# Reordering the first loads of an eight-core decoder trunk: modulation tiles in 1 MB transfers, half of x first, weight slabs gated, write-backs late

## The chip, the cores and the metric

The kernel runs on the 8 cores of one Trainium2 chip, one batch element on each core. Nothing passes between cores. The time is that of the slowest core, in microseconds (us); each quoted time of a run adds about 2 us to the span of its slowest core. Cores 0 to 3 are one die, cores 4 to 7 the other. The kernel issues its transfers from two queues, that of the SP engine and that of the POOL engine, and both use the core's 16 DMA engines (on the page of the kernel before, SP's queue takes 30.9% of their time and POOL's 20.2%).

Every execution lists the span and the mean granted TensorE clock of each core. In some executions one die, or both, are granted a lower clock and the run takes some per cent longer: the state *slow*. One run of the control took 6626 us, with cores 4 to 7 at 0.809 to 0.811; its cores 0 to 3 had 0.973 to 0.974. Fast runs are compared with fast runs. There is a second way to compare: a core shares no data with the others, so the cores of a die that was not slowed can be read even when the other die was (cores 0 to 3 of that run took 5689.7 to 5703.8 us, those of the control's two fast runs 5679.0 to 5704.1).

## The reference

Four layers, each a token mixer and a SwiGLU feed-forward, each with a modulated RMSNorm in front. What matters here is that nothing can start before the modulation of layer 0 is known, and that the modulation is a product of a vector with a 1024 x 6144 matrix.

```python
c_act = jax.nn.silu(c)                                   # (B, D)
for i in range(DEPTH):
    mod = jnp.einsum("bd,de->be", c_act, ada_w[i]) + ada_b[i]   # (B, 6D)
    sh1, sc1, g1, sh2, sc2, g2 = [m[:, None, :] for m in jnp.split(mod, 6, axis=-1)]
    h = rmsnorm(x, norm_mix_g[i]) * (1.0 + sc1) + sh1
    ...                                                  # layer 0: short gated convolution
    x = x + g1 * y
    h = rmsnorm(x, norm_ffn_g[i]) * (1.0 + sc2) + sh2
    x = x + g2 * swiglu(h, ffn_w_in[i], ffn_w_out[i])
```

## The kernel before

x is handled in four *passes* of 1024 positions, each in two halves of 512 (`nt` 0 and 1). Layer 0's mixer is ten weight slabs ("units") long; each slab serves both halves. In pass 0 a slab comes from HBM as f32, is cast to bf16 by the transfer on the POOL queue, and is written back to HBM as bf16 by the SP queue for the later passes:

```python
def load_slab(g):
    ...
    if s == 0 and (i, p) == (0, "M"):
        P.op("pool", lambda e: e.dma_start(out=wring[:, k, 0:L], in_=wsrc(i, p, q)), writes=[wb[k]], ...)
        P.op("sp", lambda e: e.dma_start(out=wdst(i, p, q), in_=wring[:, k, 0:L]), reads=[wb[k]], ...)
```

There are four slots in the ring. The modulation weights come as tiles of 128 x 512 f32 (256 KB); VectorE multiplies each with the activation and sums it (`ada_mul`). Layer 0's first two sections, 32 tiles, must be done before the first norm; the other 64 tiles of layer 0 are spread over the passes (16 in pass 0, 48 in passes 1 and 2) through a ring of three buffers. The conversions of layer 0's feed-forward weights to bf16 (`conv_tasks`, HBM to HBM, 19 slabs) are spread over the passes too. The start:

```python
issue_loads()                      # slabs 0 to 3 on POOL's queue, their write-backs on SP's
pre0[0]()                          # x, first half
for t in range(22):                # 22 modulation tiles, 256 KB each, on SP's queue
    ada_dma(0, t, hid2[...], ..., q="sp")
pre0[1]()                          # x, second half
for fn in pre0[2:12]: fn()         # squares and rstd of both halves
for t in range(22): ada_mul(0, t, ...)
for fn in ada_tasks(0, range(22, 32)): fn()    # 10 more tiles through the ring of three
...
for fn in pre0[12:]: fn()          # 16 norms
```

Of the kernel before, what the change touches and what calls it, by code (L numbers as in the profile page):

```python
# [7 lines left out]
F32 = mybir.dt.float32  # L8
# [13 lines left out]
LAG = 1  # L22
# [46 lines left out]
def _slab_table():  # L69
    tab = {}  # L70
    src = 0
    dst = 0
    for i in range(4):
        for part in (("B1", "B2", "B3", "F") if i % 3 == 1 else ("M", "F")):
            rows = []
            for name, L in _sub_slabs(i, part):
                if name == "bconv":
                    rows.append((name, L, None, dst))
                else:
                    rows.append((name, L, src, dst))  # L80
                    src += L * 128
                dst += L * 128
            tab[(i, part)] = rows
    return tab, src, dst

SLABS, TOTW, TOTB = _slab_table()
# [171 lines left out]
SECTIONS = (1, 0, 2, 4, 3, 5)  # L258
NCV = 10

def build():
# [4 lines left out]
    adaw = nc.dram_tensor("adaw", [4, NEH, 128, 512], F32, kind="ExternalInput").ap()  # L266
# [7 lines left out]
    P = Prog()  # L274
    es = contextlib.ExitStack()
    with es:
# [3 lines left out]
        xres = sb("xres", [128, 2, 8, NT], F32)  # L280
        hbuf = sb("hbuf", [128, 2, 8, NT], BF16)
        hid2 = sb("hid", [128, FC * NT], BF16)
        wring = sb("wring", [128, NRING, SLOT], BF16)
# [39 lines left out]
        xb = [[[Buf(f"x{b}_{c}_{t}") for t in range(2)] for c in range(8)] for b in range(2)]  # L323
        hb = [[[Buf(f"h{b}_{c}_{t}") for t in range(2)] for c in range(8)] for b in range(2)]
        hidb = [[Buf(f"hid{c}_{t}") for t in range(2)] for c in range(FC)]
        scrb = [Buf(f"scr{k}") for k in range(5)]
        wb = [Buf(f"w{k}") for k in range(NRING)]
        wdb = {(i, p, q): Buf(f"wd{i}{p}{q}") for (i, p), rows in SLABS.items() for q in range(len(rows))}
# [36 lines left out]
        def vcol(name, c=0, w=1):  # L365
            o = VOFF[name] + c
            return vecs[:, o:o + w]
# [35 lines left out]
        def wsrc(i, part, q):  # L403
            name, L, src, dst = SLABS[(i, part)][q]
            return wpack[src:src + 128 * L].rearrange("(p l) -> p l", p=128)

        def wdst(i, part, q):
            name, L, src, dst = SLABS[(i, part)][q]
            return wbf[dst:dst + 128 * L].rearrange("(p l) -> p l", p=128)
# [14 lines left out]
            cvstate["hist"].append(b)  # L424

        seq = []
        wstate = dict(loaded=0, used=0, done=0)

        def load_slab(g):
            i, p, s, q = seq[g]  # L430
            name, L, src, dst = SLABS[(i, p)][q]
            k = g % NRING
            if s == 0 and (i, p) == (0, "M"):
                P.op("pool", lambda e: e.dma_start(out=wring[:, k, 0:L], in_=wsrc(i, p, q)), writes=[wb[k]], sem=f"wc{k}", inc=16)
                P.op("sp", lambda e: e.dma_start(out=wdst(i, p, q), in_=wring[:, k, 0:L]), reads=[wb[k]],
                     writes=[wdb[(i, p, q)]], sem=f"wr{k}", inc=16)
            elif s == 0 and name == "bconv":
                def mkconv(e):
                    for gg in range(2):
                        ins = e.tensor_tensor(  # L440
                            wring[:, k, gg * CW:(gg + 1) * CW].rearrange("p (d c q) -> p d c q", c=32, q=4),
                            cmask[:, :].unsqueeze(1).unsqueeze(3).broadcast_to([128, NSH, 32, 4]),
                            wtab[:, 2 * q + gg, :, :].unsqueeze(2).broadcast_to([128, NSH, 32, 4]), ALU.mult)
                    return ins

                P.op("dve", mkconv, reads=[wtabb, convcb], writes=[wb[k]])
                P.op("sp", lambda e: e.dma_start(out=wdst(i, p, q), in_=wring[:, k, 0:L]), reads=[wb[k]],
                     writes=[wdb[(i, p, q)]], sem=f"wr{k}", inc=16)
            else:
                P.op("sp", lambda e: e.dma_start(out=wring[:, k, 0:L], in_=wdst(i, p, q)), reads=[wdb[(i, p, q)]],  # L450
                     writes=[wb[k]], sem=f"w{k}", inc=16)

        def issue_loads():
            while wstate["loaded"] < len(seq) and wstate["loaded"] < wstate["done"] + NRING:
                load_slab(wstate["loaded"])
                wstate["loaded"] += 1

        def next_slab():
            g = wstate["used"]
            assert wstate["loaded"] > g, ("slab not loadable", g, wstate)  # L460
            wstate["used"] += 1
            k = g % NRING
            return wring[:, k, :], wb[k]


        def ada_dma(i, t, dst, bufs, sem, q="pool"):
            eh = SECTIONS[t // 16] * 16 + t % 16
            P.op(q, lambda e: e.dma_start(out=dst, in_=adaw[i, eh]), writes=bufs, sem=sem, inc=16)  # L468

        def ada_mul(i, t, src, bufs):  # L470
            eh = SECTIONS[t // 16] * 16 + t % 16
            hf = eh % 2
            P.op("dve", lambda e: e.scalar_tensor_tensor(src, src, 1.0, cbc[:, hf * 512:(hf + 1) * 512], ALU.mult, ALU.mult,  # L473
                                                         accum_out=raw[:, eh:eh + 1]),
                 reads=[cbcb], writes=bufs + [rawb])
            if t % 16 == 15:
                mod_section(i, SECTIONS[t // 16])
# [33 lines left out]
        def ada_tasks(i, ts):  # L511
            ts = list(ts)
            out = []
            for n, t in enumerate(ts):
                def task(n=n):
                    if n == 0:
                        for m in range(min(2, len(ts))):
                            ada_feed(i, ts[m])
                    if n + 2 < len(ts):
                        ada_feed(i, ts[n + 2])  # L520
                    ada_eat()
                out.append(task)
            return out
# [435 lines left out]
        def pre_steps(st):  # L959
            part, i, s, xk, hk = st["part"], st["i"], st["s"], st["xk"], st["hk"]  # L960
            steps = []
            if part == "F":
                gs, sh, deps = der[:, i, 8:16], modT[:, i, 24:32], [derb[i][1], modb[i][3]]
            else:
                gs, sh, deps = der[:, i, 0:8], modT[:, i, 0:8], [derb[i][0], modb[i][0]]
            first = part == "M" and i == 0

            def ld(nt):
                x_load(xk, s, nt, 0, first)
                x_load(xk, s, nt, 1, first)  # L970

            def sq(nt, c):
                flush_stats(nt)
                stats_chunk(xk, c, nt)
                stats_chunk(xk, c + 1, nt)

            def hh(nt, c):
                if part == "CF":
                    norm_pool(xk, c, nt, gs, sh, deps, hk, s)
                else:  # L980
                    norm_h(xk, c, nt, gs, sh, deps, hk)

            steps.append(lambda: ld(0))
            steps.append(lambda: ld(1))
            for nt in range(2):
                for c in range(0, 8, 2):
                    steps.append(lambda nt=nt, c=c: sq(nt, c))
                steps.append(lambda nt=nt: rstd_make(nt))
            for nt in range(2):
                for c in range(8):  # L990
                    steps.append(lambda nt=nt, c=c: hh(nt, c))
            return steps

        todo = {}
# [95 lines left out]
        a, b = 2 * st3["end"], 2 * f0["end"] - 3  # L1090
# [34 lines left out]
        spread(conv_tasks([(3, "F")]), lo - 60, hi - 20)  # L1125


        issue_loads()
        st0 = sts[("M", 0, 0)]
        pre0 = pre_steps(st0)  # L1130
        pre0[0]()
        for t in range(22):
            ada_dma(0, t, hid2[:, t * 1024:(t + 1) * 1024].bitcast(F32), [hidb[t][0], hidb[t][1]], f"ah{t}", q="sp")
        pre0[1]()
        for fn in pre0[2:12]:
            fn()
        for t in range(22):
            ada_mul(0, t, hid2[:, t * 1024:(t + 1) * 1024].bitcast(F32), [hidb[t][0], hidb[t][1]])
        for fn in ada_tasks(0, range(22, 32)):
            fn()  # L1140
        P.op("dve", lambda e: e.tensor_scalar(der[:, 1, 24:32], vcol("bb1", 8, 8), 0.5, None, ALU.mult), reads=[vecsb], writes=[derb[1][3]])
        P.op("pool", lambda e: e.dma_start(out=wtab[:, :, :, :].rearrange("p a b c -> p (a b c)"), in_=convw_d[:, :]), writes=[wtabb], sem="cvw", inc=16)

# [2 lines left out]

        P.op("pool", conv_consts, writes=[convcb], sem="cvc", inc=32)
        P.op("sp", lambda e: e.dma_start(out=bones_f[:, :], in_=convc_d[:, 32:160]), writes=[bonesb], sem="cvf", inc=16)
        for fn in pre0[12:]:
            fn()  # L1150

        for idx in range(len(units) + LAG):
            if idx < len(units):
# [61 lines left out]
```

## Time and profile before

Median 5703 us. The page of the profile has PE busy 92% of the span. The loss that the change goes for is at the start: on core 0 PE is busy 492.9 of the first 626 us, and 4736.7 of the 5068 us after them. The four passes of layer 0's mixer, read from the timeline of PE and averaged over the 16 cores of two profiled fast runs:

| | us |
|---|---|
| first projection matmul | 91.0 |
| passes 0, 1, 2, 3 | 134.6, 137.3, 141.6, 121.1 |
| end of layer 0's mixer | 625.5 |
| from there to the end | 5064.0 |

512 matmuls of 216 ns are 111 us. By that, passes 0 to 2 are longer by 24, 26 and 31 us than their matmuls alone, and pass 3 by 10.

The timeline of SP's queue, core 0, kernel before (columns: start, us until the last issue of the group ended, what was issued, count; the us contain the waits in between):

```profile
1.52 0.42 SPq L396 DMA_DIRECT2D vecs_sb<-vecs  x1
12.99 20.23 SPq L435 DMA_DIRECT2D wbf<-wring  x4
33.27 1.60 SPq L614 DMA_DIRECT2D xres<-xT  x2
34.91 22.86 SPq L468 DMA_DIRECT2D hid<-adaw  x22
57.82 3.73 SPq L614 DMA_DIRECT2D xres<-xT  x2
...
118.78 0.34 SPq L435 DMA_DIRECT2D wbf<-wring  x1
119.16 1.53 SPq L614 DMA_DIRECT2D xres<-xT  x2
138.49 0.34 SPq L435 DMA_DIRECT2D wbf<-wring  x1
138.87 1.93 SPq L614 DMA_DIRECT2D xres<-xT  x2
```

SP stands behind four write-backs, each of which waits for its slab, so the first half of x is issued at 33 us and the modulation tiles from 35 us on. The chain of waits of the same core shows the same (start, us, what; "..." marks lines left out), with a wait of about 3 us for each of the last tiles, which come through the ring:

```profile
3.33 29.50 DMA wring<-wpack
...
34.91 18.06 DMA hid<-adaw
...
72.74 2.80 DMA aux<-adaw
...
85.92 0.76 DVE tmp L556
...
92.27 3.14 PE psum L627 x7
```

The same core in stretches (stretch; busy us of PE, PEld, DVE, ACT, POOL with counts; then the granted clock, the share of the DMA engines, GB/s):

```profile
20.00:40.00 20.00, 0.00 (x0) 0.00 (x0) 0.00 (x0) 0.00 (x0) 0.00 (x0) 1.00 0.99 254
40.00:60.00 20.00, 4.32 (x8) 0.84 (x8) 6.09 (x17) 7.29 (x11) 0.00 (x0) 1.00 1.00 307
60.00:80.00 20.00, 4.48 (x8) 0.84 (x8) 13.99 (x44) 6.12 (x10) 3.22 (x6) 1.00 0.73 227
80.00:100.00 20.00, 7.73 (x28) 3.16 (x29) 15.11 (x31) 11.26 (x17) 3.77 (x7) 1.00 0.36 91
100.00:120.00 20.00, 19.89 (x93) 9.03 (x94) 15.81 (x34) 2.39 (x4) 2.13 (x4) 1.00 0.39 89
```

The DMA engines are full from 20 to 60 us (share 0.99 and 1.00), until 33 us with slabs that are not yet needed, and then are more than half idle from 80 to 120 us (0.36 and 0.39). In the middle of pass 0 PE waits once for the x of pass 1, which was issued at 119 and 139 us behind two more write-backs (the last four lines of SP's queue above; timeline of PE, core 0; in brackets the idle time before and what ended it):

```profile
92.27 38.25 PE L627 MATMUL psum<-hbuf,wring 128*128 128x512 bf16 x165 [14.38 <-ACT hbuf L563]
...
145.94 1.10 PE L540 MATMUL psum<-sqr,ones_bf 128*128 128x512 bf16 x2 [9.16 <-ACT sqr L537]
```

### The profile page before, as it was taken

How to read it: one execution, taken by the hardware profiler on the slowest of the kernel's cores; microseconds unless marked ns; L12 is line 12 of the kernel's file. 1: busy time of each engine (PE TensorE's matmuls, PEld its weight loads, DVE VectorE, ACT ScalarE, POOL GpSimd, SP SyncE). 2: the span in 40 equal slices, each digit the busy share in tenths (PEclk: the TensorE clock that was granted, in tenths of full speed). 3: DMA queues.
4: the chain of work that ended last, by engine and by line, in shares of the span. 5: the costliest groups of instructions: out<-in, count | busy, mean ns of one | idle time of the engine just before them, and what ended most of it. 6: DMA issues, size and time to landing. Idle time of an engine off the chain costs nothing.

```text
span 5694.1 us, 73906 instructions; the slowest of 8 cores (5674.9 to 5694.1 us)
## 1 busy us (share of the span) xinstructions
PE 5264.6 (92%) x24528; PEld 2412.1 (42%) x24528; DVE 2461.0 (43%) x4314; ACT 1620.5 (28%) x2507; POOL 558.4 (10%) x916
## 2 busy tenths in 40 slices
PE   3889999999988888999999797979899999999998
PEld 1334444444444444444444343434344444444443
DVE  4667432332285655333224454545326663223222
ACT  2222222122234443222212323232312322323221
POOL 1111110110022111111000010101000000000000
PEclk9999999999998999999999899989999999999999
DMA  7888576854345655666442344435445543233132
GB/s 194 220 212 207 167 177 174 212 146 150 114 168 191 209 204 193 187 191 180 147 153 97 120 137 135 138 132 143 133 130 174 158 138 134 93 112 137 66 111 75
DMA packets 252179, 876.86 MB, mean 154 GB/s; under 512 B 29072, under 2 KB 62096, under 8 KB 220944
## 3 DMA queue, kind: packets, MB, share of 16 engines
q1 hardware_dynamic: 185808, 583.39, 30.9%
q0 software_dynamic: 66000, 288.75, 20.2%
q8 instruction: 205, 3.36, 0.2%
q14 instruction: 166, 1.36, 0.1%
HBM read 813.12 MB, written 219.68 MB: 181 GB/s over the span
## 4 chain that ended last, share of the span: by engine, by line
PE 81%; DVE 7%; DMA 5%; ACT 3%; issue 3%; SPq 0%; DVEq 0%; POOL 0%; ACTq 0%; POOLq 0%
PE psum L627 78%; PE psum L540 2%; DMA xres<-xT 2%; DVE tmp L556 1%; PE psum L790 1%; DMA wring<-wbf 1%; DVE aux L590 1%; DMA wring<-wpack 1%; ACT sqr L537 1%; DMA aux<-adaw 1%; ACT hbuf L563 1%; DVE xres L642 1%; DVE tmp L848 0%; DVE tmp L846 0%; ACT L546 0%
## 5 line engine op out<-in xcount | busy, mean ns | idle before, releaser
L627 PE MATMUL psum<-hbuf,wring 128*128 128x512 bf16 x15872 | 3500.6, 381 | 80.1 <-ACT hbuf L563 24.1
L627 PEld LDWEIGHTS psum<-hbuf,wring 128*128 128x128 bf16 x15872 | 1557.1, 98 | 1977.5 <-issue 138.4
L627 PE MATMUL psum<-hid,wring 128*128 128x512 bf16 x6656 | 1456.3, 379 | 8.4 <-DVE hid L695 8.4
L934 DVE TENSOR_TENSOR hid<-psum,sg 128x512 bf16<-128x512 f32 x704 | 485.1, 691 | 1772.0 <-PE psum L627 1507.3
L627 PEld LDWEIGHTS psum<-hid,wring 128*128 128x128 bf16 x6656 | 650.7, 98 | 794.8 <-issue 12.1
L933 ACT ACTIVATE sg<-psum 128x512 f32<-128x512 f32 x704 | 417.9, 596 | 1506.4 <-PE psum L627 1470.2
L642 DVE SCALAR_TENSOR_TENSOR xres<-psum,modT,xres 128x512 f32<-128x512 f32 x384 | 281.4, 748 | 628.2 <-PE psum L627 624.1
L563 ACT ACTIVATE hbuf<-tmp,modT 128x512 bf16<-128x512 f32 x448 | 313.9, 722 | 800.1 <-DVE tmp L556 799.2
L537 ACT ACTIVATE sqr<-xres 128x512 bf16<-128x512 f32 x576 | 337.3, 622 | 587.5 <-DVE xres L642 332.6
L540 PE MATMUL psum<-sqr,ones_bf 128*128 128x512 bf16 x576 | 201.6, 400 | 277.4 <-ACT sqr L537 272.1
L556 DVE SCALAR_TENSOR_TENSOR tmp<-xres,der,rstd 128x512 f32<-128x512 f32 x512 | 388.9, 788 | 16.3 <-ACT rstd L547 16.3
L618 POOL DMA_DIRECT2D xd<-xres x384 | 209.1, 545 | 1640.4 <-DVE xres L642 876.9
L468 POOL DMA_DIRECT2D aux<-adaw x362 | 195.5, 541 | 1342.3 <-DVE aux L473 1120.2
L473 DVE SCALAR_TENSOR_TENSOR aux<-aux,cbc 128x512 f32<-128x512 f32 x362 | 247.3, 683 | 116.9 <-DMA aux<-adaw 115.0
L540 PEld LDWEIGHTS psum<-sqr,ones_bf 128*128 128x128 bf16 x576 | 57.0, 99 | 392.7 <-issue 348.5
L790 PE MATMUL psum<-aux,wring 128*128 128x256 bf16 x1152 | 160.3, 292 | 37.5 <-DMA wring<-wbf 17.4
L685 ACT ACTIVATE sg<-psum 128x512 f32<-128x512 f32 x128 | 75.6, 591 | 380.0 <-PE psum L627 350.2
L686 DVE TENSOR_TENSOR aux<-psum,sg 128x512 f32<-128x512 f32 x128 | 88.6, 692 | 193.1 <-ACT sg L685 184.5
L790 PEld LDWEIGHTS psum<-aux,wring 128*128 128x128 bf16 x1152 | 118.2, 104 | 70.9 <-issue 43.8
L813 POOL TENSOR_TENSOR hid<-hid 128x512 f32<-128x512 f32 x60 | 99.6, 1660 | 410.0 <-DVE hid L797 409.5
L577 ACT ACTIVATE aux<-tmp,modT 128x512 f32<-128x512 f32 x64 | 46.2, 722 | 301.7 <-DVE tmp L556 301.7
L422 POOL DMA_DIRECT2D wbf<-wpack x93 | 47.6, 512 | 764.1 <-PE psum L627 413.4
(72 smaller groups left out, 1679.0 us busy)
## 6 DMA issues: line engine op xcount, KB each, us to landing
wring<-wbf SPq DMA_DIRECT2D x214, 1024.0 KB, 5.8
xres<-xd SPq DMA_DIRECT2D x112, 1024.0 KB, 11.4
xd<-xres POOLq DMA_DIRECT2D x384, 256.0 KB, 3.6
aux<-adaw POOLq DMA_DIRECT2D x362, 256.0 KB, 5.2
wring<-wbf SPq DMA_DIRECT2D x128, 704.0 KB, 4.3
wbf<-wpack POOLq DMA_DIRECT2D x52, 1024.0 KB, 13.1
wring<-wbf SPq DMA_DIRECT2D x56, 768.0 KB, 6.1
wring<-wbf SPq DMA_DIRECT2D x48, 576.0 KB, 5.5
```

The costliest lines, as they stand in the source:

```text
L468: P.op(q, lambda e: e.dma_start(out=dst, in_=adaw[i, eh]), writes=bufs, sem=sem, inc=16)
L473: P.op("dve", lambda e: e.scalar_tensor_tensor(src, src, 1.0, cbc[:, hf * 512:(hf + 1) * 512], ALU.mult, ALU.mult, accum_out=raw[:, eh:eh ...
L537: P.op("act", lambda e: e.activation(sqr2[:, nt, k, :], xres[:, xk, c, tsl(nt)], AF.Square), reads=[xb[xk][c][nt]], writes=[sq2b[nt][k]])
L540: P.op("pe", lambda e: e.matmul(bk, ones_bf[:, :], sqr2[:, nt, k, :], start=(c == 0), stop=(c == 7)), reads=[sq2b[nt][k], constb], writes= ...
L556: P.op("dve", lambda e: e.scalar_tensor_tensor(tmp_t[:, tk, :], xres[:, xk, c, tsl(nt)], gs[:, c:c + 1], rstd_t[:, nt, :], ALU.mult, ALU.m ...
L563: P.op("act", lambda e: e.activation(hbuf[:, hk, c, tsl(nt)], tmp_t[:, tk, :], AF.Identity, bias=sh[:, c:c + 1], scale=1.0), reads=[tmpb[t ...
L618: P.op("pool", lambda e: e.dma_start(out=xd[s, nt, c], in_=xres[:, xk, c, tsl(nt)]), reads=[xb[xk][c][nt]], writes=[xdb[s][nt][c]], sem=f" ...
L627: ins = pe.matmul(bk, slab[:, k * stride + col0:k * stride + col0 + 128], rhs_fn(k, nt), start=(k == 0), stop=(k == kchunks - 1))
L642: P.op("dve", lambda e: e.scalar_tensor_tensor(xs, bk, gvec, xs, ALU.mult, ALU.add), reads=[bkb] + deps, writes=[xb[xk][c][nt]])
L790: ins = pe.matmul(bk[:, 0:256], slab[:, par * CW + d * 128:par * CW + (d + 1) * 128], uP[:, g, 8 - d:264 - d], start=(d == 0), stop=(d == ...
L933: P.op("act", lambda e: e.activation(sg_t[:, k, :], gt, AF.Silu), reads=[gtb], writes=[sgb[k]])
L934: P.op("dve", lambda e: e.tensor_tensor(hid(hp(f), nt), up, sg_t[:, k, :], ALU.mult), reads=[upb, sgb[k]], writes=[hidb[hp(f)][nt]])
```

## The change

The intent: bring first what is needed first. The 32 modulation tiles come in eight transfers of 1 MB, into buffers that are free at that time (x's second buffer, and the hidden buffer). Four of them go ahead of x's first half, four behind it. Slab 0 may start when transfer 4 has landed, slab 1 after transfer 6, slabs 2 and 3 after transfer 7. A slab is written back at its first use instead of at its load. The second half's squares and norms go behind the first half of unit 0.

```diff
             if s == 0 and (i, p) == (0, "M"):
-                P.op("pool", lambda e: e.dma_start(out=wring[:, k, 0:L], in_=wsrc(i, p, q)), writes=[wb[k]], sem=f"wc{k}", inc=16)
-                P.op("sp", lambda e: e.dma_start(out=wdst(i, p, q), in_=wring[:, k, 0:L]), reads=[wb[k]],
-                     writes=[wdb[(i, p, q)]], sem=f"wr{k}", inc=16)
+                P.op("pool", lambda e: e.dma_start(out=wring[:, k, 0:L], in_=wsrc(i, p, q)), writes=[wb[k]],
+                     after=[gate[g]] if g in gate else [], sem=f"wc{k}", inc=16)
...                                                       (in next_slab, at the first use:)
+            i, p, s, q = seq[g]
+            if s == 0 and (i, p) == (0, "M"):
+                L = SLABS[(i, p)][q][1]
+                P.op("sp", lambda e: e.dma_start(out=wdst(i, p, q), in_=wring[:, k, 0:L]), reads=[wb[k]],
+                     writes=[wdb[(i, p, q)]], sem=f"wr{k}", inc=16)
...                                                       (the start; ada_home and ada_quad are cut)
-        issue_loads()
+        for n in range(4):
+            ada_quad(n)
         pre0[0]()
-        for t in range(22):
-            ada_dma(0, t, hid2[:, t * 1024:(t + 1) * 1024].bitcast(F32), [hidb[t][0], hidb[t][1]], f"ah{t}", q="sp")
+        landed = [ada_quad(n) for n in range(4, 8)]
+        gate.update({0: landed[0], 1: landed[2], 2: landed[3], 3: landed[3]})
+        issue_loads()
         pre0[1]()
-        for fn in pre0[2:12]:
+        for fn in pre0[2:7]:
             fn()
-        for t in range(22):
-            ada_mul(0, t, hid2[:, t * 1024:(t + 1) * 1024].bitcast(F32), [hidb[t][0], hidb[t][1]])
-        for fn in ada_tasks(0, range(22, 32)):
+        for t in range(32):
+            ada_mul(0, t, *ada_home(t))
+        for fn in pre0[12:20]:
             fn()
+        todo.setdefault(-2 * LAG, []).extend(pre0[7:12] + pre0[20:])
...
-        for fn in pre0[12:]:
-            fn()
```

More of the change, by code (lines that the diff above doesn't have):

```diff
@@ L426, in build @@
         seq = []
+        gate = {}
         wstate = dict(loaded=0, used=0, done=0)
@@ L1125, in build, with ada_home, ada_quad @@
         spread(conv_tasks([(3, "F")]), lo - 60, hi - 20)
-        issue_loads()
         st0 = sts[("M", 0, 0)]
         pre0 = pre_steps(st0)
+        def ada_home(t):
+            if t < 16:
+                return xres[:, 1, t // 2, (t % 2) * 512:(t % 2 + 1) * 512], [xb[1][t // 2][t % 2]]
+            return hid2[:, (t - 16) * 1024:(t - 15) * 1024].bitcast(F32), hidb[t - 16]
+        def ada_quad(n):
+            eh = SECTIONS[n // 4] * 16 + (n % 4) * 4
+            if n < 4:
+                dst = xres[:, 1, 2 * n:2 * n + 2, :].rearrange("p c (h t) -> p (c h) t", h=2)
+            else:
+                dst = hid2[:, (4 * n - 16) * 1024:(4 * n - 12) * 1024].bitcast(F32).rearrange("p (a t) -> p a t", t=512)
+            bufs = [b for t in range(4 * n, 4 * n + 4) for b in ada_home(t)[1]]
+            P.op("sp", lambda e: e.dma_start(out=dst, in_=adaw[0, eh:eh + 4].rearrange("a p t -> p a t")), writes=bufs, sem=f"ah{n}", inc=16)
+            m = Buf("gate")
+            m.w = {f"ah{n}": P.cnt[f"ah{n}"]}
+            return m
+        for n in range(4):
+            ada_quad(n)
         pre0[0]()
-        for t in range(22):
-            ada_dma(0, t, hid2[:, t * 1024:(t + 1) * 1024].bitcast(F32), [hidb[t][0], hidb[t][1]], f"ah{t}", q="sp")
+        landed = [ada_quad(n) for n in range(4, 8)]
+        gate.update({0: landed[0], 1: landed[2], 2: landed[3], 3: landed[3]})
+        issue_loads()
         pre0[1]()
-        for fn in pre0[2:12]:
+        for fn in pre0[2:7]:
             fn()
-        for t in range(22):
-            ada_mul(0, t, hid2[:, t * 1024:(t + 1) * 1024].bitcast(F32), [hidb[t][0], hidb[t][1]])
-        for fn in ada_tasks(0, range(22, 32)):
+        for t in range(32):
+            ada_mul(0, t, *ada_home(t))
+        for fn in pre0[12:20]:
             fn()
+        todo.setdefault(-2 * LAG, []).extend(pre0[7:12] + pre0[20:])
         P.op("dve", lambda e: e.tensor_scalar(der[:, 1, 24:32], vcol("bb1", 8, 8), 0.5, None, ALU.mult), reads=[vecsb], writes=[derb[1][3]])
```

## The prediction

> **What bounds the kernel.** The page shows PE busy 92% of 5694 us. But PE's first projection matmul runs at 93.84 us (timeline), and the chain's first pieces are transfers: wring<-wpack 31.57 us, hid<-adaw 17.50, three aux<-adaw of about 3, then DVE norms. SP issues four weight write-backs first, and each waits for its slab, so x is issued only at 35.3 us and adaw at 36.9. VectorE's first modulation product runs at 54.45; 32 of them at about 0.81 us, with ring waits, end at 86.8. Normalising then takes 6.3 us to the first matmul. DMA is 0.92 to 0.99 busy up to 60 us, then 0.71, 0.38 and 0.36 to 120 us: first the wrong bytes, then idle.
>
> Layer 0's mixer is also held up by transfers: its four passes take about 134, 135, 142 and 120 us (PE timeline), where 512 matmuls at 216 ns are 111 us. After that PE is 95 to 99% busy, so what is gained by then should stay.
>
> **What the change does.** Same matmuls, same bytes. 32 modulation tiles come as eight 1 MB transfers, four before x's first half, four after; slab 0 starts when transfer 4 lands, slab 1 after 6, slabs 2 and 3 after 7; write-backs move to first use. The second half's statistics and norms move behind unit 0's first half.
>
> **Cost.** Before the first matmul must land: 0.8 MB constants, 4.2 MB adaw, 2.1 MB x, 4.2 MB adaw and slab 0 (1.6 MB as f32): 12.8 MB. The DMA windows show 299 GB/s in 40 to 60 us, slices up to 344[...]. At 320 GB/s (estimate) that is 40 us, plus about 4 of start and latency: last tile at 44 to 46 us. VectorE keeps pace (1 MB in 3.3 us, four products 3.2). Tail: 3.2 + 0.6 + 6.3. First matmul at 54 us (50 to 60), gain about 39 us.
>
> Given back: after the first 24 matmuls (5.2 us) PE waits behind the second half's squares, which ScalarE starts only after unit 0's copy (squares and rstd took 7.5 us at 72.9 to 80.3), then behind its eight norms: about 8 us in two gaps. Gained: x for pass 1, now issued at 120 and 141 us, goes at about 70, which removes some of the 12 us of waits in pass 0. Against that, slabs, write-backs, x and adaw want about 15 MB in the 43 us after 57 us[...], so slabs 4 to 6 may come a few us late. I expect pass 0 to last about as long as now (130 to 138), and passes 1 to 3 unchanged: their transfers are tied to the same units.
>
> So 5703 - 38 = 5665 us. Range 5646 to 5684. Chances: faster by over 2% 0.01, within 2% 0.98, slower 0.01.
>
> **What would show it.** First product by 12 us; last at 43 to 50; first projection near 54; DMA above 0.9 until 120 us; a gap of 4 to 6 us after PE's first 24 matmuls; end of layer 0's mixer at about 587 instead of 625; everything later shifted as a block.
>
> **What would make it wrong.** Slab 0's cast transfer slowing the last adaw transfers more than its share; first matmul after 65 us; DMA backlog stretching passes 0 to 2, since x loads there already took up to 43 us (chain); or, on the good side, passes 1 and 2 losing their x waits too.

40 us for 12.8 MB at 320 GB/s and 4 of start and latency make 44, taken as 44 to 46; with a tail of 10.1 the first matmul comes at 54, about 39 us earlier than at 93.84, and the forecast keeps 38 of them (5703 - 38 = 5665). The 320 is the estimate between the 299 and 344 read from the trace (which shows more over short stretches: 370 GB/s from 52 to 56 us on core 0); the 4 us are an estimate too (in the kernel before SP issues its first transfer at 1.08 us on core 0, and a 256 KB transfer from SBUF takes 3.6 us to landing, the median of the page). The 15 MB in the 43 us after 57 us would be 349 GB/s; that slabs then come late was an estimate as well, and core 0 of the changed kernel moved 10.11 MB from 57 to 100 us. One reading was too good: after the mixer PE of core 5 is busy 100% of the time up to 1400 us, but 83 to 100% in each stretch of 400 us from there to 5400.

## The result

Median 5701.22 us against 5705.02. The ratio of the fast runs is 0.9988, with a 95% interval of 0.9965 to 1.0011. (A ratio is the mean time of one kernel's fast runs over that of the other's of the same rounds, so it is not quite the ratio of the medians quoted.) The prediction was 5665, with a range of 5646 to 5684: wrong. A gain of 38 us was foretold, and 4 came by these medians (7 by the means of the fast runs, 5704.1 and 5697.3). The verdict within 2% was right.

But the start did change much. SP's queue on core 0 of the changed kernel, same view as above:

```profile
1.97 4.87 SPq L1148 DMA_DIRECT2D xres<-adaw  x4
6.88 7.68 SPq L619 DMA_DIRECT2D xres<-xT  x2
14.60 17.27 SPq L1148 DMA_DIRECT2D hid<-adaw  x4
31.91 12.44 SPq L619 DMA_DIRECT2D xres<-xT  x2
47.91 18.84 SPq L466 DMA_DIRECT2D wbf<-wring  x3
66.85 19.00 SPq L619 DMA_DIRECT2D xres<-xT  x4
```

The modulation weights are issued from 2 us on, and the x of pass 1 at 67 us instead of 119. The stretches of the same core:

```profile
20.00:40.00 20.00, 4.32 (x8) 0.84 (x8) 8.33 (x26) 7.29 (x11) 0.68 (x1) 1.00 0.99 297
40.00:60.00 20.00, 0.00 (x0) 0.00 (x0) 13.12 (x34) 3.88 (x6) 4.82 (x9) 1.00 1.03 250
60.00:80.00 20.00, 8.59 (x30) 3.18 (x30) 4.19 (x10) 5.41 (x10) 0.00 (x0) 0.86 1.01 226
80.00:100.00 20.00, 18.16 (x74) 7.47 (x74) 13.51 (x26) 9.59 (x15) 1.84 (x3) 0.88 0.83 253
100.00:120.00 20.00, 19.96 (x93) 8.93 (x92) 16.44 (x38) 3.98 (x7) 3.93 (x7) 1.00 0.87 222
```

The engines are no longer idle between 80 and 120 us. The timeline of PE, core 0:

```profile
61.63 6.66 PE L632 MATMUL psum<-hbuf,wring 128*128 128x512 bf16 x24 [25.30 <-ACT hbuf L568]
...
79.35 1.10 PE L545 MATMUL psum<-sqr,ones_bf 128*128 128x512 bf16 x2 [9.08 <-ACT sqr L542]
...
81.70 6.88 PE L632 MATMUL psum<-hbuf,wring 128*128 128x512 bf16 x24
90.07 26.06 PE L632 MATMUL psum<-hbuf,wring 128*128 128x512 bf16 x120 [1.49 <-ACT hbuf L568]
...
230.25 18.03 PE L632 MATMUL psum<-hbuf,wring 128*128 128x512 bf16 x72 [10.96 <-DVE aux L691]
...
286.33 22.48 PE L632 MATMUL psum<-hbuf,wring 128*128 128x512 bf16 x96 [6.00 <-DMA wring<-wbf]
```

The first projection comes 31 us earlier than before (61.63 against 92.27). Then there are three things to see: a gap of 9.08 us before the second half; 24 matmuls that take 6.88 us afterwards instead of the 5.34 that such a group takes at a clock of 1.00 (at 116.62 us); and, in pass 1, two gaps of 11 and 6 us. The kernel before waits in pass 1 too, but elsewhere: 3.24 and 5.62 us ahead of squares, for x.

A low clock came with the gap: core 0 was granted 0.50 between 75 and 80 us and 0.52 between 80 and 85, and 1.00 again from 85 to 95.

The gap of 10.96 us in pass 1 is reported behind a VectorE instruction, but VectorE itself had been standing behind a modulation tile. Two lines of the view of waits in pass 1 (us in total, times, longest), the kernel before first:

```profile
DVE aux L473 <- DMA aux<-adaw: 13.6, 4, 6.6
```

and the changed kernel:

```profile
DVE aux L478 <- DMA aux<-adaw: 30.4, 7, 15.0
```

And there is something that no part of the prediction had. The view of the cores of the changed kernel's profiled run, second die:

```profile
core 4: 5681.9 us, clock 0.973
core 5: 5687.6 us, clock 0.973
core 6: 5696.8 us, clock 0.968
core 7: 5682.4 us, clock 0.969
```

Stretches of core 6 and then of core 4 in the same execution:

```profile
100.00:140.00 40.00, 38.59 (x146) 15.59 (x145) 25.20 (x57) 12.42 (x22) 5.87 (x11) 0.81 0.70 195
140.00:200.00 60.00, 59.29 (x226) 24.38 (x225) 40.31 (x78) 15.88 (x25) 7.14 (x14) 0.81 0.62 149
```

```profile
100.00:140.00 40.00, 37.55 (x169) 16.50 (x170) 29.17 (x66) 14.28 (x25) 6.51 (x13) 1.00 0.87 207
140.00:200.00 60.00, 58.56 (x266) 26.44 (x272) 46.26 (x86) 15.89 (x25) 10.12 (x19) 1.00 0.77 185
```

Cores 6 and 7 were granted 0.81 from about 85 to 240 us, read in steps of 5 us (1.00 from 245); cores 4 and 5, of the same die, 1.00 from 100 to 200. By that clock a core does the work of 130 us in 160 (an estimate: 160 x 0.81). I call this an *episode*: both cores of a pair (0 and 1, 2 and 3, and so on) with a mean clock at least about 0.003 under the level of the same kernel's other cores, on a die that is not slow. Five of the seven fast runs of the changed kernel (its two jobs together) have one, and in all five the slowest core is one of such a pair.

So two questions: where did an undisturbed core's gain go, and what is the episode? Averages over cores that saw no low clock up to the end of layer 0's mixer, from the profiled runs (us; "cores" is how many were averaged):

| kernel | cores | first matmul | pass 0 | pass 1 | pass 2 | pass 3 | mixer ends |
|---|---|---|---|---|---|---|---|
| before | 16 | 91.0 | 134.6 | 137.3 | 141.6 | 121.1 | 625.5 |
| changed | 12 | 60.1 | 139.6 | 143.9 | 141.8 | 121.4 | 606.7 |
| changed, in an episode | 4 | 59.3 | 162.2 | 134.4 | 141.4 | 124.0 | 621.4 |
| half2_first | 6 | 82.9 | 126.5 | 143.9 | 142.3 | 120.5 | 616.1 |
| wb_late_only | 8 | 98.0 | 126.4 | 141.4 | 142.1 | 120.7 | 628.5 |
| x2_first | 14 | 60.1 | 138.3 | 142.2 | 143.0 | 120.9 | 604.4 |
| conv_late | 4 | 60.0 | 139.4 | 119.0 | 172.5 | 142.5 | 633.4 |
| balanced | 4 | 57.7 | 154.9 | 131.8 | 130.8 | 120.9 | 596.1 |
| before_spread3 | 8 | 92.5 | 135.5 | 126.9 | 129.0 | 121.7 | 605.5 |
| after_spread3 | 4 | 60.6 | 137.4 | 132.7 | 129.3 | 120.9 | 581.0 |
| x2_spread3 | 14 | 59.7 | 135.7 | 130.2 | 129.4 | 121.2 | 576.3 |

An undisturbed core thus gains 30.9 us at the first matmul, gives back 5.0 in pass 0 and 6.6 in pass 1, and has 18.8 left at the end of the mixer. Over all executions the median span of undisturbed cores is 5691.0 before (200 core spans) and 5674.4 changed (40): 16.6 us. The slowest core of an undisturbed die goes from 5698.4 to 5680.1 (medians). The rest of the gain is hidden by episodes.

### The profile page after: what moved, and what is told of

The parts are those of the page before. It is cut to its first block, busy times and chain, and to the rows that moved or that the text cites. A ratio compares the mean times of both kernels' runs of the same rounds, so it can differ in the third digit from the quotient of the medians.

```text
span 5696.8 us, 73844 instructions; the slowest of 8 cores (5666.5 to 5696.8 us)
## 1 busy us (share of the span) xinstructions
PE 5290.1 (93%) x24528; PEld 2417.9 (42%) x24528; DVE 2463.4 (43%) x4314; ACT 1620.2 (28%) x2507; POOL 552.1 (10%) x906
## 4 chain that ended last, share of the span: by engine, by line
PE 80%; DVE 7%; DMA 5%; ACT 3%; issue 3%; SPq 1%; DVEq 0%; POOL 0%; ACTq 0%; POOLq 0%
PE psum L632 77%; PE psum L545 2%; DMA wring<-wbf 2%; DMA xres<-xT 1%; DVE tmp L561 1%; DVE aux L595 1%; DMA aux<-adaw 1%; DVE xres L647 1%; PE psum L795 1%; ACT sqr L542 1%; ACT hbuf L568 1%; ACT aux L582 1%; DVE tmp L853 0%; DVE tmp L851 0%; SPq L1148 0%
## 5 line engine op out<-in xcount | busy, mean ns | idle before, releaser
L422 POOL DMA_DIRECT2D wbf<-wpack x93 | 47.5, 511 | 777.3 <-PE psum L632 422.8
```

## The experiments

All kernels gave correct results. Each number of a pass below is from the table above. Theories: **DMA** says that the lost gain went to transfers in each other's way; **throttle** says that it went to the low clock.

### Control: the kernel before

> The kernel before, unchanged, as a control. Two theories for why the change gave 0.1% and not 0.7%. Theory DMA: the start gained 28 to 34 us, and 8 to 10 us each come back in pass 0 (gap before the second half) and pass 1 (transfers in each other's way). Theory throttle: in the changed kernel's profiled run a pair of cores (6 and 7) was granted 0.81 from about 82 to 244 us, and another run shows low clocks on cores 0, 1, 6 and 7, which makes the slowest core late. If the throttle comes with the change, this control has all eight clocks within 0.002 of each other (0.973 to 0.975) in every fast run, and no core at 0.81 for over 100 us in its trace. If it is chance of the chip, some pair here shows 0.968 too. Time 5700 to 5706.

Measured: the two fast runs took 5704.0 and 5706.0 us, all clocks 0.974 to 0.976, and in the trace no core is held at 0.81 within layer 0's mixer. The executions of the kernel before beside it do have episodes, but few: in all jobs together 6 of 56 dies that were not slow. So an episode is not special to the change; its frequency is in question.

### The changed kernel, counted

> The changed kernel, unchanged, to count episodes of low clock. So far a pair or a die below 0.972 showed in 2 of 3 of its fast runs and in 2 of 8 fast runs of the kernel before. If the change draws them, most fast runs here show a pair at 0.968 to 0.970 and the ratio stays at 0.998 to 1.000. If they are chance, about a quarter of the runs show one, the fast runs without one lie at 5685 to 5692 us, and the ratio comes to 0.996 to 0.998. Spans of cores at 0.973 or more: median 5675 to 5680, against 5688 to 5695 in the kernel before, either way.

Measured: ratio 0.999 (0.9965 to 1.0015). Three of its four fast runs had an episode (5695.9, 5696.1 and 5701.8 us), one had none (5680.7). In both jobs together: fast runs without an episode 5680.7 and 5689.4 us, with one 5695.9 to 5704.1. In the expectation of x2_first_again, further down, I had counted 8 of 16 dies, by a looser rule (any core at 0.971 or lower); by the rule for pairs it is 6 of 16. The expectation of "most runs, ratio 0.998 to 1.000" held. So the flat ratio has two parts: about 17 us of gain on undisturbed cores, and episodes that take most of it from the slowest core again. The second part is read from few runs: the five with an episode have a mean of 5699.2 us, the two without one 5685.1.

### The second half of x ahead of slabs 2 and 3

```diff
-        gate.update({0: landed[0], 1: landed[2], 2: landed[3], 3: landed[3]})
-        issue_loads()
         pre0[1]()
+        xh2 = Buf("gate")
+        xh2.w = {k: P.cnt[k] for k in ("xl010", "xl011")}
+        gate.update({0: landed[0], 1: landed[2], 2: xh2, 3: xh2})
+        issue_loads()
```

> The changed kernel with slabs 2 and 3 gated on the second half of x instead of on the last modulation transfer. Theory DMA[...]: it lands at 60 to 65 us, the gap of 9 us after the first 24 matmuls falls to 3 to 4, pass 0 on a core with full clock goes from 142 to 134 to 137 us, and the end of layer 0's mixer moves by up to 6 us if pass 1 does not take it back. Rival (the gap comes from the order of the ScalarE and VectorE work, not from the landing): the gap stays over 7 us. Time 5685 to 5698.

(The theory is that the half landed late, at 78 us on core 0, because of other transfers.)

Measured: the two slabs, and with them the proof that the second half had landed, go at 60.9 us on core 0, where the changed kernel got the half at 78.4 (chain of waits: 42.97 us from 35.41, when SP turned to the issue of its second piece; 26.80 us in x2_first). PE, core 0:

```profile
59.28 7.72 PE L632 MATMUL psum<-hbuf,wring 128*128 128x512 bf16 x24 [24.88 <-ACT hbuf L568]
...
71.47 6.78 PE L632 MATMUL psum<-hbuf,wring 128*128 128x512 bf16 x23
79.84 26.06 PE L632 MATMUL psum<-hbuf,wring 128*128 128x512 bf16 x118 [1.59 <-ACT hbuf L568]
```

The gap of 9.08 us is gone; the rival falls. The third group starts at 79.84 instead of 90.07. That these 10 us are not kept is seen in the table: pass 0 only falls from 139.6 to 138.3 (136.8 in this run alone), because later waits in the same pass take the place of the gap (PE of core 0 is busy 18.73 us from 100 to 120 us where the changed kernel has 19.96, and 55.88 instead of 58.21 from 140 to 200). The fast runs took 5676, 5682 and 5686 us (ratio 0.9932, interval 0.9867 to 0.9997; its other side contains the run of 5765 under a lower clock), better than expected. No die had an episode.

Why did the half land late? It was in SP's queue by 44 us with nothing ahead of it but the last modulation transfers, which had landed by 51.5 us. But slabs 1 to 3 and the first ring tiles were in POOL's queue at the same time: from 51.5 to 78.4 us the engines of core 0 took 938 packets (3.01 MB) from POOL's queue and 954 (3.05 MB) from SP's. How the engines choose between the queues is not shown. These shares and the two landings show what counts here: its place in SP's queue did not put the half ahead of POOL's transfers (landed by 78.4), the gate did (60.9).

> x2_first once more, to count. It starts PE in one go with the DMA engines full. Theory burst: again no pair at 0.968 to 0.971 (0 of 6 dies so far, against 8 of 16 for the changed kernel). Theory load: about half the dies that are not slow show one. Fast runs 5676 to 5688 us, cores at 0.973 or more with a median near 5672.

Measured: no episode again, now 0 of 13 dies; the one fast run took 5678.2 us. Median of undisturbed cores in both jobs 5672.7.

### The second half's work back in front

```diff
-        for fn in pre0[2:7]:
+        for fn in pre0[2:12]:
...
-        for fn in pre0[12:20]:
+        for fn in pre0[12:]:
             fn()
-        todo.setdefault(-2 * LAG, []).extend(pre0[7:12] + pre0[20:])
```

> The changed kernel with the second half's squares and norms back ahead of unit 0, as before the change. Theory: the first projection matmul moves from about 60 to about 88 us (landing of the second half at 78 plus squares, rstd and 16 norms), the gap after 24 matmuls is gone, and the end of pass 0 comes 5 to 10 us later than in the changed kernel. Theory throttle, bursts: the pair at 0.81 comes from PE starting in short bursts with gaps; here PE starts once and runs on, as before the change, so no core shows 0.968. Rival: the throttle comes from the chip's state or from cores starting together, and pairs at 0.968 show here as often as in the changed kernel (2 of 3 fast runs). Time 5690 to 5705.

Measured: first matmul at 82.9 us and the end of pass 0 at 209.4 instead of 199.7 (first matmul plus pass 0), so 9.7 us later, as expected. Starting after half of x brings the first matmul 22.8 us forward and costs 13.1 us of pass 0, and the net gain is 9.4 us at the end of the mixer. That is half of the change's gain; the other half (616.1 against 625.5) is the loads. One fast run was undisturbed (5695.3); in the profiled fast run (5754.4) cores 2 and 3 were at 0.81 from 85 us on with breaks to 545 us. So an episode also comes without the burst start: 1 of 7 dies.

### Late write-backs alone

The edit is the first part of the diff on the kernel before, without the gate: the write-back moves from `load_slab` to `next_slab`.

> The kernel before with the late write-backs alone: x and the modulation tiles are issued from 2 us on, still as 22 small transfers and 10 through the ring, and the four slabs still start at 1.6 us. Theory (the loss at the start was the wrong bytes first): four slabs (6.3 MB as f32) share the engines with x and the tiles, so the first projection matmul comes at 68 to 80 us, between 60 and 91. Rival (the loss was SP waiting for slabs, nothing else): it comes at 60 us or earlier. End of layer 0's mixer 3 to 12 us earlier than in the kernel before; time 5690 to 5703.

Measured: 98.0 us. Both theories missed: it starts *later* than the kernel before. SP's queue on core 0:

```profile
1.98 0.98 SPq L617 DMA_DIRECT2D xres<-xT  x2
3.00 43.21 SPq L471 DMA_DIRECT2D hid<-adaw  x22
46.25 3.90 SPq L617 DMA_DIRECT2D xres<-xT  x2
...
56.47 16.42 SPq L617 DMA_DIRECT2D xres<-xT  x4
```

No write-back stands at the head of SP's queue any more, so from 56 us on it issues the 4 MB of x for pass 1, which nobody needs before 130 us. The last ten tiles of the modulation go through a ring of three on the other queue, and two of the waits for them now take 10 to 11 us instead of 3 (core 1, chain of waits, kernel wb_late_only):

```profile
60.46 10.25 DMA aux<-adaw
...
72.13 11.19 DMA aux<-adaw
```

Pass 0 is then 8.2 us shorter (x for pass 1 is there), the start 7 us later, and pass 1 4.1 us longer: nothing gained (one fast run, 5705.9; undisturbed cores 5694.2 against 5691.0). As I read it, the wait at the head of SP's queue in the kernel before was a brake, and also an accidental order; that x for pass 1 is what slows the last tiles was not tested by itself.

Note pass 1 in the table: 143.9, 143.9 and 141.4 us in the three kernels with late write-backs and pass 0's gap or none, against 137.3 before, whether PE started at 60, 83 or 98 us. So the loss in pass 1 does not come from the early start. It comes with the new order of pass 0's transfers. Which of them does it, I did not take apart.

### Conversions out of pass 1

```diff
-        spread(conv_tasks([(0, "F")]), lo + 14, hi - 8)
+        spread(conv_tasks([(0, "F")]), lo + 40, hi - 8)
```

> The changed kernel with layer 0's feed-forward weight conversions held back to the start of pass 2. Theory DMA: pass 1 loses its waits for aux<-adaw and wring<-wbf (11 and 6 us on core 0) and falls from 144 to 118 to 126 us; passes 2 and 3 grow, since the same conversions now fall there in 32 instead of 58 positions, by 10 to 25 us together. Rival (pass 1's waits come from the x loads and the ring alone): pass 1 stays above 136 us. Time 5680 to 5705.

Measured: pass 1 takes 119.0 us on all four cores read, and VectorE's wait for tiles of adaw in it, 30.4 us in the changed kernel, is all but gone (view of waits, core 0):

```profile
DVE aux L478 <- DMA aux<-adaw: 0.2, 1, 0.2
```

Passes 2 and 3 together grow by 52 us, far more than expected, and the fast runs took 5744 and 5774 us. The profiled run was slow, but the four cores read (0, 1, 4, 5) had no stretch at 0.81 before 750 us. This shows what pass 1 waits for: the 25 us over the bare 119 go when the conversions go, and the share of the DMA engines in pass 1 falls from 0.87 to 0.60 (core 0). The rival falls. Whether the conversions take the engines' time, or stand ahead of the tiles in POOL's queue, from which both are issued, this run does not separate. It is a peak of demand that wanders, not a fixed cost.

### The same work, spread thinner

```diff
-        spread(ada_tasks(0, range(48, 96)), *span("M", 0, 1, 3))
+        spread(ada_tasks(0, range(48, 96)), span("M", 0, 1, 3)[0], span("M", 0)[1])
...
-        spread(conv_tasks([(0, "F")]), lo + 14, hi - 8)
+        spread(conv_tasks([(0, "F")]), lo + 5, hi - 8)
```

> The changed kernel with the conversions of layer 0's feed-forward weights spread from unit 2 or 3 of pass 0 on (instead of unit 7), and the 48 later modulation tiles over passes 1 to 3 instead of 1 and 2. Theory DMA (passes 1 and 2 ask for more than the engines move, passes 0 and 3 for less): pass 1 from 144 to 128 to 138 us, pass 2 from 142 to 128 to 138, pass 0 up by 0 to 6, pass 3 from 121 to 121 to 126; layer 0's mixer ends 8 to 20 us earlier than in the changed kernel, at 592 to 602. Rival (the sum of the work, not its distribution, sets the end): the mixer still ends at 607 to 612. Time 5668 to 5682 in fast runs without a low clock.

Measured: passes 1 and 2 131.8 and 130.8 us, the mixer ends at 596.1, both as expected. Pass 0 rose to 154.9, more than the 6 us allowed: pass 0 had no room for conversions after all. Fast runs 5678.4 and 5680.5, ratio not available (too few fast runs beside it), and an episode on 5 of 6 dies.

> Both: slabs 2 and 3 gated on the second half of x, and the conversions and tiles spread as in the run called balanced. If the two gains are separate (start, and passes 1 and 2), they add: about 5 us better than balanced, mixer ends at 587 to 598, time 5662 to 5678. If pass 0 is then full, its first slabs come late and the gain of one eats that of the other: no better than balanced alone.

Measured: no fast run in six, so no time to compare. On the four cores without a low clock the mixer ends at 591.4 us on average (585.5 to 596.6), within the expectation, with a pass 0 of 148 to 160 us. An episode on 2 of 3 dies that were not slow.

Spreading to the back instead of to the front, since layer 0's feed-forward takes its slabs one after another:

```diff
-        spread(ada_tasks(0, range(48, 96)), *span("M", 0, 1, 3))
+        spread(ada_tasks(0, range(48, 96)), span("M", 0, 1, 3)[0], span("M", 0)[1])
...
-        spread(conv_tasks([(0, "F")]), lo + 14, hi - 8)
+        spread(conv_tasks([(0, "F")]), lo + 14, hi + 10)
```

> x2_first with the later work spread thinner: 48 modulation tiles over passes 1 to 3 instead of 1 and 2, and the feed-forward conversions from unit 7 of pass 0, as in the changed kernel, to ten positions into the next stage instead of eight before its start. Theory DMA: pass 0 stays at 134 to 142 (balanced, which began them earlier, had 152 to 157), passes 1 and 2 fall from about 143 to 124 to 134 each, pass 3 stays at 120 to 124: mixer ends at 583 to 594, against 600 to 608 in x2_first. Rival: the conversions that are left in the next stage stall it, and the end comes no earlier than in x2_first. Time without a low clock 5655 to 5670.

Measured: pass 0 135.7, pass 1 130.2, pass 2 129.4, the mixer ends at 576.3, better than expected. One fast run, 5658.0 us.

> The kernel before with that spread alone. If the two are separate, it gains what x2_spread3 gains on x2_first, 10 to 20 us (mixer ends at 603 to 613, 5682 to 5693 us). If the spread only pays where the start came early, it gains under 5 us.

Measured: passes 1 and 2 126.9 and 129.0, the mixer ends at 605.5, the one fast run took 5690.7; undisturbed cores 5674.5 against 5691.0. So this small edit of two lines gains an undisturbed core on the kernel before as much (16.5 us) as the whole reordering of the start (16.6). Which of the two lines does it, no run separates. Together with x2_first the two add, and a little more: 5649.1, 41.9 us under the kernel before, where x2_first alone has 18.3.

> x2_spread3 once more for a verdict: fast runs 5655 to 5662 us, 0.7 to 0.8% under the kernel before; cores at 0.973 or more with a median of 5649; no pair at 0.968 to 0.971.

Measured: one fast run again, 5661.0 us. The two fast runs, 5658.0 and 5661.0, have a mean of 5659.5; the six fast runs of the kernel before in the same two jobs (5699.7 to 5708.1) have 5702.7: 0.9924, without an interval, since there was one fast run in each job. The 48 undisturbed core spans in both jobs (median 5649.1) say the same. No episode on 12 dies. By the core spans this version beats both kernels; by run times alone, two fast runs are few.

### What draws the episode?

Two theories: a second slow start of PE after a gap (burst), or PE starting while the DMA engines are full (load). The expectation calls the slow start cold; what is seen on core 0 of the changed kernel is 0.50 granted from 75 to 80 us and 24 matmuls in 6.88 us instead of 5.34. before_gap gives the kernel before a gap, with engines that have little to do:

```diff
+                 after=[marker("pe")] if first and s == 0 and nt == 1 else [],      # x_load: the second half waits for unit 0
...
-        for fn in pre0[12:]:
+        for fn in pre0[12:20]:
             fn()
+        todo.setdefault(-2 * LAG, []).extend([pre0[1]] + pre0[7:12] + pre0[20:])
```

> The kernel before with its second half of x loaded, squared and normed only after unit 0's first 24 matmuls: a start in two bursts with a gap of over 8 us, as in the changed kernel, but with the DMA engines nearly idle around it. Theory burst (a second cold start of PE draws the low clock): a third or more of the dies that are not slow show a pair at 0.968 to 0.971 and the trace shows 0.81 from about 120 us on. Theory load (PE starting while the DMA engines are full draws it): none or one, as in the kernel before (2 of 32 dies so far). Time without a low clock 5700 to 5720.

Measured: PE stands for 6.1 us before the squares on core 0 (shorter than expected) and was granted 0.51 from 100 to 110 us; the DMA share there is 0.39. No episode on 6 dies; ratio 1.0035 (1.0012 to 1.0058). That speaks against burst alone, though six dies are few: if a third of the dies had episodes, none in six would still come up about once in eleven. x2_first, full engines (0.97 from 60 to 80 us on core 0) and no gap of 9 us, has 0 of 13, which speaks against load alone. That left the two together:

```diff
+        def stall():
+            for n in range(14):
+                P.op("act", lambda e: e.activation(sqr2[:, 1, 0, :], xres[:, 0, 0, tsl(0)], AF.Square),
+                     reads=[xb[0][0][0]], writes=[sq2b[1][0]])
+
+        todo.setdefault(-2 * LAG, []).extend([stall] + pre0[7:12] + pre0[20:])
```

> x2_first with 14 idle squares on ScalarE (about 9 us) ahead of the second half's squares: PE again stands still for 8 to 10 us after its first 24 matmuls, while the DMA engines are full, with the loads in the order of x2_first. Theory gap with full engines: a pair at 0.968 to 0.971 in a third or more of the dies that are not slow. Rival (something else in the order of the loads): none or one. Time without a low clock 5682 to 5694.

Measured: a gap of 9.72 us on core 0, with a DMA share of 0.98 in the stretch from 60 to 80 us, and no episode on 6 dies (one fast run, 5689.3 us). That speaks against the theory "gap with full engines" as well, again on six dies.

> The changed kernel with the thinner spread alone, slabs 2 and 3 gated as the change has them. Dies without a low clock: cores with a median of 5650 to 5658 (x2_spread3 has 5649, the changed kernel 5672). Theory gap with full engines: its start is the changed kernel's, so a pair with a low clock shows in a third or more of the dies that are not slow, and the slowest core is 10 to 20 us later there. Rival (the later load matters): none.

Measured: passes as in x2_spread3, undisturbed cores 5650.9, within the expectation, and one episode on 4 dies, which decides nothing between the two; its only run that counts as fast (5987 us) had a clock of 0.92 on all cores and is not used.

All counts, dies that were not slow:

| kernel | episodes |
|---|---|
| before | 6 of 56 |
| wb_late_only, before_gap, before_spread3 | 0 of 4, 0 of 6, 0 of 5 |
| half2_first | 1 of 7 |
| changed, after_spread3, conv_late, balanced | 6 of 16, 1 of 4, 3 of 4, 5 of 6 |
| x2_balanced | 2 of 3 |
| x2_first, x2_gap, x2_spread3 | 0 of 13, 0 of 6, 0 of 12 |

The kernels that start PE on half of x and gate slabs 2 and 3 on the last tiles have 15 of 30; those that gate them on the second half of x have 0 of 31, or 2 of 34 with x2_balanced. Jobs ran on several chips. Within one job there is one clear contrast, conv_late 3 of 4 beside x2_first 0 of 6 (1 of 4 for after_spread3 beside 0 of 6 for x2_gap says little), and the changed kernel never ran in one job with x2_first.

These counts leave out the slow dies, and that matters. In the profiled slow run of x2_first_again, cores 0 and 1 were at 0.81 from 85 us to beyond 2000 us while cores 2 and 3 had 1.00 from 100 to 200 us; cores 6 and 7 in that of x2_spread3 were the same. That is how an episode begins, only it did not end. With the slow dies counted too, the first group has a low clock on 35 of 50 dies, the second (without x2_balanced) on 31 of 62, and the kernel before on 44 of 94. So on dies that were not slow the episodes go with the order of the loads, and neither a gap nor full engines were seen to draw them. That the order draws the low clock itself is not shown. What does remains open.

## Why the prediction was wrong

- **Right:** PE stood idle for the wrong bytes, and reordering brings the first matmul forward by tens of us; the end of the mixer shifts and the rest keeps the shift. From there to the end it is 5064.0 us before and 5067.2 changed on the averaged cores.
- **The start: too few bytes in the sum.** The prediction had "at 320 GB/s (estimate) that is 40 us, plus about 4 of start and latency: last tile at 44 to 46 us". On core 0 the last modulation transfer let VectorE go on at 51.5 us, and the first matmul came at 60.1 on average, not at 54. The prediction's 12.8 MB count slab 0 as the 1.6 MB of f32 that it reads; the profile counts the 0.79 MB that it writes, which makes 12.0 MB. By 51.5 us the engines of core 0 had moved 13.88 MB. So about 1.8 MB more were moved first than the sum had, by the order of the issues above all x's second half, which SP issued from 31.9 us on. With slab 0 as f32 that is 14.7 MB in 47.5 us (51.5 less the estimated 4), 309 GB/s: the rate was nearly right. By the profile's own count, over all of the 51.5 us, it is 270 GB/s. This term of the sum, the bytes that land first, was mis-sized by about 6 us. Another 3 us were never there, since 39 counts from the 93.84 us of one core, and the average is 91.0. The tail of 10 us behind the last tile was right.
- **"about 8 us in two gaps"** was of the right kind and too small: 9.08 and 1.49 us on core 0, and the next 24 matmuls in low clock (0.52 from 80 to 85 us). The prediction had derived the gap from ScalarE's work and assumed that the data were there; x2_first shows that it was the landing of the second half at 78 us, pushed back by slabs that the prediction had taken as harmless.
- **"I expect pass 0 to last about as long as now (130 to 138), and passes 1 to 3 unchanged: their transfers are tied to the same units"** failed. Pass 0 took 139.6, pass 1 143.9 instead of 137.3. Transfers are tied to units in the order of issue, but what PE waits for them hung on what else was issued: in conv_late, without the conversions, the same pass takes 119.0. The risk was named ("DMA backlog stretching passes 0 to 2"), but given no us.
- **The step that was missing.** All sums were for one core at full clock, and the metric is the slowest of eight. Episodes of a low clock came on 6 of 16 dies of the changed kernel, against 6 of 56 before; in the mixer they cost the averaged pair cores 14.7 us (621.4 against 606.7), not the 22.6 of pass 0 alone, since pass 1 was shorter on those cores (134.4 against 143.9). In it VectorE waited 10.0 us for tiles of adaw on core 6 and 26.8 on core 4, in the same execution.

Sum for an undisturbed core: 30.9 gained at the start, 5.0 and 6.6 given back in passes 0 and 1, 0.5 in passes 2 and 3, leaves 18.8 at the end of the mixer, instead of 38. The run's time then loses most of it again to episodes. What the episodes come from, and which transfer makes pass 1 longer than before, is open.

Of the signs that the prediction named, on core 0: the first product came at 12.55 us (by 12), the last ended at 54.5 (43 to 50), the DMA share was 0.83 and 0.87 after 80 us (above 0.9 until 120), the gap was 9.08 us (4 to 6). The mixer ended at 606.7 on average (587).

## What to carry to other kernels

An early start is only worth what the next stages can keep: where the same transfers wait further on, look at those stages first. Here two lines that spread later traffic thinner were worth as much as the whole new start, and the two gains added. Here the place in SP's queue did not put the half of x ahead of POOL's transfers (3.05 MB against 3.01 from 51.5 to 78.4 us), and a gate brought it from 78.4 to 60.9 us: gate what is not needed yet on the landing of what is, and expect that a wait you remove may have been holding back transfers that you did not want (wb_late_only started at 98.0 us instead of 91.0). Before a small difference of an eight-core kernel is explained, read every core's clock in every run, and compare undisturbed cores. And when events are counted on a part of the runs, look at what was left out.
